# One pool of eight PSUM banks for the whole first phase, and the sample group's products in float32 in quarters of TensorE's columns

## The chip, the core and the metric

The kernel runs on one core of a Trainium2 chip. The metric is the device time of one execution in microseconds (us). The work is spread over TensorE (PE, matmuls and transposes; PEld is its weight load), VectorE (DVE), ScalarE (ACT), GpSimd (POOL) and the queues that issue transfers. TensorE writes its results into PSUM, which has eight banks; a bank holds 128 partitions by 512 float32 values.

## The reference

One step of a two-layer decoder. Layer 0 is sparse attention: an indexer scores all earlier positions, the 256 best are kept, and attention runs over those alone. Layer 1 is a gated linear recurrence (RG-LRU). Two groups go through both layers: a prompt of 2048 tokens, and a sample group of 8 sequences with 4 new tokens each (32 rows), whose 16384 past positions lie in a paged cache.

```python
def attn_project(h, pos, w_in, q_norm, k_norm):
    z = h @ w_in                       # (tokens, 1024) @ (1024, 3664)
    q, k, v, qi, ki, wi, g = jnp.split(z, offs, axis=-1)
    ...
def indexer_select(qi, wi, ki, q_pos, k_sel):
    dots = jnp.einsum('thd,ld->thl', qi, ki)
    score = jnp.einsum('th,thl->tl', wi, jax.nn.relu(dots))
    ...
    _, idx = lax.top_k(score, k_sel)
...
out = (hs * jax.nn.silu(g)) @ w_out    # end of layer 1, (tokens, 1024) @ (1024, 1024)
```

Both groups use the same weights, so each weight matrix is multiplied with 2048 prompt rows and with 32 sample rows.

## The kernel before

The program has three phases. In phase A all tokens are projected by `attn_w_in` (1024 by 3664). The columns are cut into eight groups (`GROUPS`, 384, five times 512, twice 360 columns), the prompt into two halves of eight tiles of 128 tokens. For each group `load_w` fetches the weights (`wraw`), and splits them into a rounded part `whi` and a rest `wlo`; the tokens are split into `hhi` and `hlo` in the same way. A product in full precision is then three fast matmuls (`mm3`: whi with hhi, wlo with hhi, whi with hlo), summed over eight blocks of rows: 24 matmuls into one bank, named `zps`. `make_h` builds hhi and hlo from the prompt's rows: a load (`x`, three buffers), a square sum, two scalings, eight transposes (`htr`).

The sample group has its own chain at the head of phase A. `sample_in` multiplies its rows with the first three groups (`szps`); `sample_scores` then works through 16384 cached indexer keys for each of 8 sequences: 64 gathers of 512 KB (`s_raw`, two buffers), each of them cut into two rounds of four transposes (`s_tp`), a copy by ScalarE (`s_kT`), four products (`s_dots`) and two passes of VectorE (`s_r`, `SC`), 128 rounds in all. `sample_threshold` (names with `st_`) finds the 256th best score by a few steps of a search, and `sample_select` (names with `ss_`, the last matmuls are `ss_ohps`) lists the chosen positions. Only after these three does the program text come to `project`, which holds the prompt's products; into it `weave` lets the sample's attention (`attend`, names with `sa_`), the second layer's conditioning (`ada1`, `aps`) and the first indexer blocks of the prompt (`dots`) in at given shares of its progress.

The order on each engine isn't written by hand. A scheduler places the instructions by their place in the program, and lets a later one go ahead when the earlier ones wait for their inputs; an instruction that writes a new tile needs a free buffer of that tile's pool and tag. The banks of phase A are dealt out like this, by pools and tags:

```python
pps = es.enter_context(tc.tile_pool(name="a_ps", bufs=2, space=PSUM))       # z: 2 banks, tr: 1
pss = early.enter_context(tc.tile_pool(name="a_ps1", bufs=3, space=PSUM))   # st: 3, sd: 2, sample chain
    ps = pps.tile([P, 512], F32, tag="z", name="zps")                       # prompt's projection
    tp = pps.tile([P, 4, P], F32, tag="st", name="s_tp")                    # sample_scores, its pps is a_ps1
```

The pool a_ps1 is followed by a_ps2 for `attend` and by a_ps3 and a_ps4 for the indexer, five banks each.

Phase B is the prompt's attention; its last part (`first_chunk`) also starts layer 0's output product (`ops`, and `sops` for the sample rows). Phase C is the recurrence, in four chunks of 512 tokens. In the first of them each product has a companion for the sample rows: `columns` (`sps`, input weights), `sample_gate` inside `gates` (`sps`, the two gate matrices, fed by `sample_lru`'s `sl_xh` and `sl_xl`), and `row_gemm` in `lru_out` (`sops`). All of these are `mm3` with 32 columns of stationary operand, one after the other with the prompt's matmuls. `load_split` gives their weights, with three (phase B) or four (phase C) buffers of `wraw`.

Of the kernel before, what the change touches and what calls it, by code (L numbers as in the profile page):

```python
# [22 lines left out]
P = 128  # L23
# [47 lines left out]
def _constants():  # L71
# [13 lines left out]
    c["tk_c"] = cf  # L85
    c["iota9"] = np.tile(np.arange(9, dtype=np.float32), (P, 1))
# [7 lines left out]
    for order in (  # L94
        ["ident", "causal", "tk_z", "tk_c", "tk_h", "iota9"],
        ["s_lt", "s_nm", "s_rt", "s_slot", "iota256"],
    ):
# [102 lines left out]
def setup(k, ctx, tc):  # L200
# [21 lines left out]
    k.ogT = [k.cp.tile([P, H, RS], F32R, tag=f"ogT{j}", name=f"ogT{j}") for j in range(2)]  # L222
# [88 lines left out]
def load_w(k, src, row_stride, c0, w, wpool, engs, sub):  # L311
# [3 lines left out]
    for kk in range(0, KT, 2):  # L315
# [7 lines left out]
        out.append((hi, lo))  # L323
    return out

# [64 lines left out]
def sample_h(k, li, x, pool, pps, tag, ptag="tr", mod=None):  # L390
# [22 lines left out]
    hi = k.pp.tile([P, KT, RS], F32R, tag=f"{tag}hi", name=f"{tag}hi")  # L413
    lo = k.pp.tile([P, KT, RS], F32R, tag=f"{tag}lo", name=f"{tag}lo")
    split_ps(k, hi, lo, ps)
    return hi, lo
# [15 lines left out]
def sample_evac(k, gi, ps, pool):  # L432
    nc = k.nc
    a, b = GROUPS[gi]
    if gi == 0:
        z = k.s_ki
        nc.scalar.copy(z[:, 0, :], ps[:, 0:ID])
        nc.scalar.mul(k.s_w, ps[:, WI0 - a : WI0 - a + IH], 1.0 / 32.0)
# [3 lines left out]
    elif gi in (1, 2):  # L442
        z = k.s_qi[:, (gi - 1) * 8 : gi * 8, :]
        nc.scalar.copy(z, ps.rearrange("p (h d) -> p h d", d=ID))
        rope(k, nc.gpsimd, z, 8, ID, k.rope_s, pool, RS)
        return
    elif gi in (3, 4, 5):
# [3 lines left out]
        nc.scalar.copy(z, ps.rearrange("p (h d) -> p h d", d=HD))  # L451
# [20 lines left out]
    nc.scalar.activation(g[:, :n], ps[:, off : off + n], AF.Silu, bias=0.0, scale=1.0)  # L472
# [359 lines left out]
def sample_attend(k, pool, pps):  # L832
# [67 lines left out]
    def output(b, s_ps, vs):  # L900
# [41 lines left out]
        og = pool.tile([P, 2, 4, TD], F32, tag="sa_og", name="sa_og")  # L942
        g = tr["g"][:, :, bt].rearrange("p (v h) t -> p v h t", v=2)
        for kv in range(2):
            V.tensor_tensor(og[:, kv], ot[:, kv, :, 0:4].rearrange("p t h -> p h t"), g[:, kv], ALU.mult)
        og = og.rearrange("p v h t -> p (v h) t")
        nc.scalar.copy(k.ogT[0][:, :, bt], og)
        V.tensor_tensor(k.ogT[1][:, :, bt], og, k.ogT[0][:, :, bt].bitcast(F32), ALU.subtract)
# [38 lines left out]
def phase_a(k):  # L987
    nc, tc = k.nc, k.tc
    with ExitStack() as es:
# [17 lines left out]
        pps = es.enter_context(tc.tile_pool(name="a_ps", bufs=2, space=PSUM))  # L1007
# [13 lines left out]
        with tc.tile_pool(name="a_hs", bufs=1, side="right") as hsp:  # L1021
# [5 lines left out]
            with tc.tile_pool(name="a_ada", bufs=2, side="right") as ap, tc.tile_pool(name="a_pb", bufs=3, space=PSUM) as pss:  # L1027
                cond_t(k, ap, pps)
                for _ in ada(k, 0, ("s", "b"), 512, ap, pps, "z", (10, 3), mod, pss):
                    pass  # L1030
# [13 lines left out]
        early = ExitStack()  # L1044
        pss = early.enter_context(tc.tile_pool(name="a_ps1", bufs=3, space=PSUM))
# [12 lines left out]
        early.close()  # L1058
# [3 lines left out]
        def project():  # L1062

            for hf in range(2):
# [7 lines left out]
                for gi, (a, b) in enumerate(GROUPS):  # L1072
# [4 lines left out]
                    for tiles in TOGETHER:  # L1077
                        ps = [pps.tile([P, 512], F32, tag="z", name="zps")[:, : b - a] for _ in tiles]
                        for kk in range(KT):
                            wk = [t[:, kk % 2, : b - a] for t in w[kk // 2]]  # L1080
# [20 lines left out]
        def index():  # L1101
# [539 lines left out]
def load_split(k, wpool, src, i, bufs=(5, 10)):  # L1641
# [9 lines left out]
    nc.gpsimd.tensor_tensor(lo, raw, hi.bitcast(F32), ALU.subtract)  # L1651
    return hi, lo
# [18 lines left out]
def sample_out(k, li, ps, sl, x, y, pool):  # L1671
# [4 lines left out]
    nc.vector.tensor_tensor(g, ps, g, ALU.mult)  # L1676
# [18 lines left out]
def sample_lru(k, nb, ps_in, gemm_gate, pool):  # L1695
# [9 lines left out]
    xh, xl = t("xh", F32R), t("xl", F32R)  # L1705
# [10 lines left out]
    V.tensor_copy(xh, xc)  # L1716
    V.tensor_tensor(xl, xc, xh.bitcast(F32), ALU.subtract)
    ps_ri = gemm_gate((xh, xl))
# [20 lines left out]
    V.tensor_tensor(gg, gg, i, ALU.mult)  # L1739
    V.tensor_copy(k.s_uT[0][:, fs, :], gg)  # L1740
    V.tensor_tensor(k.s_uT[1][:, fs, :], gg, k.s_uT[0][:, fs, :].bitcast(F32), ALU.subtract)
# [63 lines left out]
def first_chunk(k, pps, tag, spool, mpool):  # L1805
# [9 lines left out]
    with tc.tile_pool(name="c_w0", reuse_waits="tile", bufs=2, side="right") as pool:  # L1815
# [9 lines left out]
        for c in range(0, D, 256):  # L1825
# [3 lines left out]
            pss = pps.tile([P, 512], F32, tag=tag, name="sops")[:RS, :256]  # L1829
            for k0 in range(0, KT, 2):  # L1830
                w = load_split(k, pool, wblock(k.a["attn_w_out"], D, k0, c, 2, 256), k0 // 2, (3, 3))
                for kk in (k0, k0 + 1):
# [5 lines left out]
                    mm3(k, pss, (k.ogT[0][:, kk, :], k.ogT[1][:, kk, :]), wk, kk == 0, kk == KT - 1)  # L1838
# [13 lines left out]
def phase_c(k):  # L1852
    nc, tc = k.nc, k.tc
    V = nc.vector
    with ExitStack() as es:
# [8 lines left out]
        k.s_uT = [one.tile([P, KT, RS], F32R, tag=f"s_u{n}", name=f"s_u{n}") for n in "hl"]  # L1864
# [282 lines left out]
```

## Time and profile before

| | before |
|---|---|
| median of 3 runs (lowest to highest), us | 3037.86 (3033.24 to 3044.44) |
| the profiled execution: its time, its span, us | 3037.36, 3035.6 |
| mean granted TensorE clock | 0.964 |
| busy: PE, PEld, DVE, ACT, POOL | 93%, 78%, 70%, 54%, 41% |
| moved by DMA | 314 MB, 103 GB/s |

The span is what the trace covers; 1.8 us of the execution lie around it. Busy shares are means over stages with different limits, and a matmul's end is modelled: matmuls overlap, so the spacing of their starts is what one costs in a stream, not its duration.

### The profile page before, as it was taken

What the parts mean: (1) busy time and instruction counts of PE and PEld (TensorE: products, weight loads), DVE (VectorE), ACT (ScalarE), POOL (GpSimd) and SP (SyncE); (2) the same over time, 40 slices, a digit from 0 to 9 for tenths busy, and PEclk for the clock granted to TensorE, in tenths of its full rate; (3) what the DMA queues carried; (4) which work ended last, traced back from release to release, by engine and by line L of the source; (5) the groups of instructions that cost most, each with busy time, mean ns of one, the idle gap of its engine ahead of it and who ended that gap; (6) DMA issues with size and microseconds to landing.
All of it is one profiled execution on the core that took longest, in us unless ns stands there. A gap on an engine that the chain in (4) does not pass through costs nothing. (4 is left out here: it accounts for less than half of the span.)

```text
span 3035.6 us, 46937 instructions
## 1 busy us (share of the span) xinstructions
PE 2837.9 (93%) x16289; PEld 2380.2 (78%) x16289; DVE 2115.0 (70%) x4600; ACT 1643.0 (54%) x3083; POOL 1241.8 (41%) x1277
## 2 busy tenths in 40 slices
PE   7999998899999998899999999999997998998998
PEld 2999886687677896788878888888775787787886
DVE  6765568945555876886888787634586487487587
ACT  5533332454443566777877776644464365365364
POOL 2644435515761542422342332124433643653643
PEclk7999999899999998999999999999998999999999
DMA  7554421145663113100110111143322522623523
GB/s 245 185 164 157 148 87 51 59 128 170 205 204 109 64 62 96 58 25 19 39 31 27 31 43 32 53 131 107 111 67 87 198 92 94 204 92 95 177 87 105
DMA packets 202014, 314.13 MB, mean 103 GB/s; under 512 B 25651, under 2 KB 119487, under 8 KB 201758
## 3 DMA queue, kind: packets, MB, share of 16 engines
q1 hardware_dynamic: 151482, 213.72, 22.3%
q0 software_dynamic: 15792, 51.92, 5.6%
q10 hardware_dynamic: 34484, 45.34, 4.6%
q8 instruction: 129, 2.11, 0.3%
q14 instruction: 127, 1.04, 0.1%
HBM read 254.56 MB, written 56.34 MB: 102 GB/s over the span
## 5 line engine op out<-in xcount | busy, mean ns | idle before, releaser
L1651 POOL TENSOR_TENSOR wlo<-wraw,whi 128x512 fp32r<-128x512 f32 x288 | 408.9, 1430 | 477.7 <-ACT whi L1650 430.8
L1230 DVE SCALAR_TENSOR_TENSOR score<-relu,sg_all,score 128x512 f32<-128x512 f32 (+2 forms) x494 | 362.3, 736 | 82.7 <-ACT relu L1222 63.4
L331 PE MATMUL zps<-whi,hhi 128*128 128x512 f32 (+2 forms) x1024 | 389.9, 382 | 15.0 <-ACT z_q L365 9.8
L332 PE MATMUL zps<-wlo,hhi 128*128 128x512 f32 (+2 forms) x1024 | 388.5, 380 | 0.0
L333 PE MATMUL zps<-whi,hlo 128*128 128x512 f32 (+2 forms) x1024 | 387.4, 379 | 0.0
L1222 ACT ACTIVATE relu<-dots 128x512 f32<-128x512 f32 (+2 forms) x608 | 314.5, 551 | 133.7 <-PE dots L1219 76.2
L1455 PE MATMUL o_ps<-v,pt 128*128 128x128 f32 x2176 | 300.9, 278 | 7.4 <-ACT pt L1467 6.7
L1650 ACT CAST whi<-wraw 128x512 fp32r<-128x512 f32 x288 | 175.2, 618 | 242.7 <-PE ops L333 112.1
L1455 PEld LDWEIGHTS o_ps<-v,pt 128*128 128x128 f32 x2176 | 284.6, 193 | 25.5 <-ACT pt L1467 11.6
L1218 PE MATMUL dots<-ki_hi,qiT 128*128 128x512 f32 (+2 forms) x608 | 248.9, 412 | 13.7 <-ACT relu L1222 11.1
L331 PEld LDWEIGHTS zps<-whi,hhi 128*128 128x128 f32 x1024 | 195.7, 191 | 49.3 <-ACT z_q L365 11.9
L1219 PE MATMUL dots<-ki_lo,qiT 128*128 128x512 f32 (+2 forms) x608 | 226.6, 374 | 0.0
L332 PEld LDWEIGHTS zps<-wlo,hhi 128*128 128x128 f32 x1024 | 195.8, 191 | 28.1 <-issue 1.2
L333 PEld LDWEIGHTS zps<-whi,hlo 128*128 128x128 f32 x1024 | 195.5, 191 | 28.1 <-issue 0.8
L1467 ACT COPY pt<-pt_ps 128x512 f32<-128x512 f32 (+3 forms) x320 | 163.7, 527 | 82.4 <-PE pt_ps L1465 77.2
L331 PE MATMUL zps<-hhi,whi 128*128 128x512 f32 x512 | 201.3, 393 | 1.2 <-ACT whi L1650 1.2
L332 PE MATMUL zps<-hlo,whi 128*128 128x512 f32 x512 | 200.9, 392 | 0.0
L333 PE MATMUL zps<-hhi,wlo 128*128 128x512 f32 x512 | 199.2, 390 | 0.0
L189 POOL TENSOR_TENSOR rs<-ms,mhalf 128x1 f32<-128x1 f32 (+4 forms) x85 | 82.3, 970 | 283.3 <-DVE ms L188 274.0
L1442 ACT ACTIVATE sp<-sp,neg 128x128 f32<-128x128 f32 (+15 forms) x128 | 154.3, 1207 | 66.7 <-POOL neg L1441 64.9
L1465 PE MATMUL pt_ps<-const,sp 128*128 128x128 f32 x1088 | 173.0, 274 | 3.6 <-ACT sp L1442 3.1
L555 ACT COPY s_kT<-s_tp 128x512 f32<-128x512 f32 x128 | 75.1, 587 | 165.7 <-PE s_dots L564 134.4
(584 smaller groups left out, 7271.0 us busy)
## 6 DMA issues: line engine op xcount, KB each, us to landing
wraw<-in_lru_w_in SPq DMA_DIRECT2D x128, 256.0 KB
wraw<-in_attn_w_out SPq DMA_DIRECT2D x64, 256.0 KB
wraw<-in_lru_w_out SPq DMA_DIRECT2D x64, 256.0 KB
wraw<-in_attn_w_in SPq DMA_DIRECT2D x28, 512.0 KB
wraw<-in_attn_w_in ACTq DMA_DIRECT2D x20, 512.0 KB
ada_raw<-in_ada_w SPq DMA_DIRECT2D x16, 512.0 KB
qi_d<-z_qi SPq DMA_DIRECT2D x32, 256.0 KB
q_d<-z_q SPq DMA_DIRECT2D x32, 256.0 KB
```

What stands on the lines that cost most here:

```text
L331: mm(ps, ah, bh, start=start, stop=False)
L332: mm(ps, ah, bl, start=False, stop=False)
L333: mm(ps, al, bh, start=False, stop=stop)
L1218: nc.tensor.matmul(ps[:, :w], q, k.ki_hi[:, c : c + w], start=True, stop=False)
L1219: nc.tensor.matmul(ps[:, :w], q, k.ki_lo[:, c : c + w], start=False, stop=True)
L1222: nc.scalar.activation(r[:, :w], ps[:, :w], AF.Relu, bias=0.0, scale=1.0)
L1230: eng.scalar_tensor_tensor(acc, r[:, :w], sg, acc, ALU.mult, ALU.add)
L1455: nc.tensor.matmul(u.o[:, j, :], pt[:, i, :], k.v_sb[k0 + i][:, u.kv * HD : (u.kv + 1) * HD], start=(k0 + i == 0), stop=(k0 + i == u.qt),)
L1465: nc.tensor.transpose(pt_ps[:, i, :], sp[:, (k0 + i) * P : (k0 + i + 1) * P], k.ident)
L1467: nc.scalar.copy(pt[:, :n, :], pt_ps[:, :n, :])
L1650: nc.scalar.copy(hi, raw)
L1651: nc.gpsimd.tensor_tensor(lo, raw, hi.bitcast(F32), ALU.subtract)
```

## The change

All PSUM tiles of phase A come from one pool of eight buffers. A small class `Banks` passes every request on under the one tag `bank`; the three extra pools are gone. The sample group's rows stay in float32 (`hsT`, `ogT`, `s_uT` lose their split halves), and so do the weights that they meet (`wraw` itself, which is kept until its product has been taken). `mm_rows` makes four matmuls of a quarter of the columns each, which write to partitions 0, 32, 64 and 96 of one bank; in `columns` and `sample_gate` the four quarters are two blocks of rows times two halves of the columns, or two matrices times two halves. What evacuates such a bank does it in four pieces, or by one matmul that sums and transposes (`s_sel`).

```diff
-        out.append((hi, lo))
+        out.append((hi, lo, raw))
+def mm_rows(k, ps, rows, w, start, stop):
+    n = w.shape[1] // 4
+    for q in range(4):
+        k.nc.tensor.matmul(ps[q * RS : (q + 1) * RS, :n], rows, w[:, q * n : (q + 1) * n], start=start, stop=stop)
...
 def sample_in(k, gi, w, pool, pps):
     a, b = GROUPS[gi]
-    hi, lo = k.hsT
-    pst = pps.tile([P, 512], F32, tag="z", name="szps")
-    ps = pst[:RS, :]
+    ps = pps.tile([P, 512], F32, tag="z", name="szps")
     for kk in range(KT):
-        wh, wl = w[kk // 2]
-        mm3(k, ps[:, : b - a], (hi[:, kk, :], lo[:, kk, :]), (wh[:, kk % 2, : b - a], wl[:, kk % 2, : b - a]), kk == 0, kk == KT - 1)
+        mm_rows(k, ps, k.hsT[:, kk, :], w[kk // 2][2][:, kk % 2, : b - a], kk == 0, kk == KT - 1)
...
-        pps = es.enter_context(tc.tile_pool(name="a_ps", bufs=2, space=PSUM))
+        pps = Banks(es.enter_context(tc.tile_pool(name="a_ps", reuse_waits="tile", bufs=8, space=PSUM)), 8)
...
-        early = ExitStack()
-        pss = early.enter_context(tc.tile_pool(name="a_ps1", bufs=3, space=PSUM))
+        pss = pps
...
         def attend():
-            with (
-                tc.tile_pool(name="a_sa", reuse_waits="tile", bufs=2, side="right") as ssp,
-                tc.tile_pool(name="a_ps2", reuse_waits="tile", bufs=2, space=PSUM) as pss,
-            ):
-                yield from sample_attend(k, ssp, pss)
+            with tc.tile_pool(name="a_sa", reuse_waits="tile", bufs=2, side="right") as ssp:
+                yield from sample_attend(k, ssp, pps)
...
-            with (
-                tc.tile_pool(name="a_ps3", reuse_waits="tile", bufs=4, space=PSUM) as pd,
-                tc.tile_pool(name="a_ps4", reuse_waits="tile", bufs=1, space=PSUM) as pq,
-            ):
-                for i in range(0, NT, 4):
-                    prep_index(k, i, pq, "q")
-                    yield 1024
-                yield from indexer(k, tiles, GP_HEADS[0], k.first, k.ip, k.ip, k.ip, "scoreA", pd, "dots", "q", pq)
+            for i in range(0, NT, 4):
+                prep_index(k, i, pps, "q")
+                yield 1024
+            yield from indexer(k, tiles, GP_HEADS[0], k.first, k.ip, k.ip, k.ip, "scoreA", pps, "dots", "q")
...
-                    mm3(k, pss, (k.ogT[0][:, kk, :], k.ogT[1][:, kk, :]), wk, kk == 0, kk == KT - 1)
+                    mm_rows(k, pss, k.ogT[:, kk, :], raw[:, kk - k0, :], kk == 0, kk == KT - 1)
...
-                    mm3(k, pss[:RS, :], (sample[0][:, kk, :], sample[1][:, kk, :]), w[kk], kk == 0, kk == KT - 1)
+                    mm_rows(k, pss, sample[:, kk, :], k.raw[:, 0, :], kk == 0, kk == KT - 1)
...
-                    if u.sample:
-                        mm3(
-                            k, u.sps[:RS, part * 256 : part * 256 + 256], (k.hsT[0][:, kk, :], k.hsT[1][:, kk, :]),
-                            [t[:, kk - k0, :] for t in w], part + kk == 0, part * kk == KT - 1,
-                        )
+                if u.sample:
+                    for j in range(2):
+                        for n in range(2):
+                            p0 = (j * 2 + n) * RS
+                            nc.tensor.matmul(
+                                u.sps[p0 : p0 + RS, part * P : (part + 1) * P], k.hsT[:, k0 + n, :],
+                                raw[:, n, j * P : (j + 1) * P], start=(k0 == 0), stop=(k0 == KT - 2),
+                            )
...
+class Banks:
+    def __init__(self, pool, n):
+        self.pool, self.n = pool, n
+    def tile(self, shape, dt, tag=None, name=None, bufs=None):
+        return self.pool.tile(shape, dt, tag="bank", name=name, bufs=self.n)
```

On TensorE, in the middle of the scoring (`sample_scores`), the order before has the prompt's `zps` between the sample's rounds:

```order
L331 MATMUL zps<-whi,hhi 128x512
L553 MATMUL s_tp<-const,s_raw 128x128
L564 MATMUL s_dots<-bd,s_kT 128x128 x4
L553 MATMUL s_tp<-const,s_raw 128x128 x2
L564 MATMUL s_dots<-bd,s_kT 128x128 x4
L553 MATMUL s_tp<-const,s_raw 128x128 x5
L332 MATMUL zps<-wlo,hhi 128x512
L333 MATMUL zps<-whi,hlo 128x512
```

In the changed kernel the same place, the start of the scoring on TensorE, reads (the line numbers have moved by some 13):

```order
L334 MATMUL szps<-wraw,hs_474 32x128 x8
L514 MATMUL s_qps<-const,s_qi 128x32 x12
L545 MATMUL s_nps<-bd,s_kn 4x64 x8
L566 MATMUL s_tp<-const,s_raw 128x128 x8
L577 MATMUL s_dots<-bd,s_kT 128x128 x4
L566 MATMUL s_tp<-const,s_raw 128x128 x4
L577 MATMUL s_dots<-bd,s_kT 128x128 x4
```

The last two rows go on in turn to the end of the 128 rounds, and no `zps` and no `htr` stands between them.

At the end of the selection on TensorE, the order before again alternates; `ss_oh` and `ss_ohps` are the sample's, `zps` the prompt's:

```order
L818 LDWEIGHTS ss_oh
L818 MATMUL ss_ohps<-ss_R,ss_oh 128x130
L331 MATMUL zps<-whi,hhi 128x360
L332 MATMUL zps<-wlo,hhi 128x360
L333 MATMUL zps<-whi,hlo 128x360
L331 MATMUL zps<-whi,hhi 128x360
L332 MATMUL zps<-wlo,hhi 128x360
L818 LDWEIGHTS ss_oh
L818 MATMUL ss_ohps<-ss_R,ss_oh 128x130
```

In the changed kernel the last `ss_ohps` is followed by the transposes of the first eight prompt tiles, and then by the first `zps` of the program:

```order
L831 LDWEIGHTS ss_oh
L831 MATMUL ss_ohps<-ss_R,ss_oh 128x130
L308 MATMUL htr<-const,x 128x128 x64
L341 MATMUL zps<-whi,hhi 128x384
L342 MATMUL zps<-wlo,hhi 128x384
L343 MATMUL zps<-whi,hlo 128x384
```

The prompt's projection has moved behind the sample's whole chain. The 64 transposes of the second half of the prompt (`htr`) likewise stand in one block behind the last `zps` of the first half, where before they alternated with that half's last `zps`.

In phase C, chunk 0, TensorE's order before has three matmuls for the sample (`sps`) behind each six of the prompt:

```order
L333 MATMUL zps<-hhi,wlo 128x512
L331 MATMUL sps<-whi,hs1hi 32x256
L332 MATMUL sps<-wlo,hs1hi 32x256
L333 MATMUL sps<-whi,hs1lo 32x256
L331 MATMUL zps<-hhi,whi 128x512
```

In the changed kernel four quarter matmuls (`hs` is the sample's rows in float32) stand behind each twelve of the prompt:

```order
L343 MATMUL zps<-hhi,wlo 128x512
L1941 MATMUL sps<-wraw,hs_27539 32x128 x4
L341 MATMUL zps<-hhi,whi 128x512
```

Six matmuls with 256 columns have become four with 128.

## Rows read from the trace of the kernel before

**Rows 1.** The page: busy time of the engines, TensorE's granted clock in 40 slices
```profile
PE 2837.9 (93%) x16289; PEld 2380.2 (78%) x16289; DVE 2115.0 (70%) x4600; ACT 1643.0 (54%) x3083; POOL 1241.8 (41%) x1277
PEclk7999999899999998999999999999998999999999
```

**Rows 2.** Busy time of each engine by stretch, with granted clock and DMA
```profile
core 0: us, PE busy (x) PEld busy (x) DVE busy (x) ACT busy (x) POOL busy (x), PEclk, DMA share, GB/s
...
98.00:425.00 327.00, 326.52 (x2260) 297.60 (x2257) 204.45 (x334) 113.85 (x207) 134.67 (x174) 1.00 0.47 147
425.00:500.00 75.00, 71.52 (x308) 53.34 (x308) 56.16 (x230) 23.38 (x35) 42.95 (x51) 0.98 0.26 80
500.00:634.00 134.00, 111.21 (x566) 89.73 (x565) 121.56 (x256) 65.52 (x217) 61.98 (x55) 0.90 0.19 59
...
2110.00:2330.00 220.00, 185.33 (x949) 146.50 (x948) 158.25 (x272) 122.94 (x216) 85.85 (x62) 0.91 0.27 87
```

**Rows 3.** The same view for the tile zps alone, 75 to 634 us
```profile
75.00:634.00 559.00, 333.56 (x1398) 253.55 (x1399) 1.33 (x8) 33.86 (x74) 0.97 0.39 120
```

**Rows 4.** Groups of instructions, 98 to 425 us: count, busy us, mean ns, idle before
```profile
L572 DVE TENSOR_REDUCE SC<-s_r 128x32 f32<-128x512 f32 x128 | 87.9, 688 | 4.0
L570 DVE SCALAR_TENSOR_TENSOR s_r<-s_dots,s_wb 128x512 f32<-128x512 f32 x128 | 87.8, 687 | 101.4 <-PE s_dots L564 100.8
```

**Rows 5.** TensorE's instructions in order of time, one round of the scoring
```profile
300.67 0.40 PE L333 MATMUL zps<-whi,hlo 128*128 128x512 f32 x1
300.91 0.27 PE L553 MATMUL s_tp<-const,s_raw 128*128 128x128 f32 x1
301.02 1.06 PE L564 MATMUL s_dots<-bd,s_kT 128*128 128x128 f32 x8
301.91 0.38 PE L553 MATMUL s_tp<-const,s_raw 128*128 128x128 f32 x2
```

**Rows 6.** DMA issues: engine, count, median us from issue to landing
```profile
x<-in_x_prompt POOLq DMA_DIRECT2D x3, 512.0 KB, 5.0
s_raw<-in_cache_idx_k,s_idx POOLq DMA_INDIRECT x64, 4.6
```

**Rows 7.** Groups of VectorE, 425 to 500, then 500 to 634; ScalarE, 574 to 634
```profile
L375 DVE SCALAR_TENSOR_TENSOR z_q<-z_q,rs,qn 128x128 f32<-128x128 f32 x24 | 7.5, 370 | 0.2 <-POOL rs L189 0.2
L371 DVE TENSOR_REDUCE ssq<-sq 128x4 f32<-128x512 f32 (+1 forms) x9 | 5.3, 588 | 7.5 <-ACT sq L369 7.5
...
L375 DVE SCALAR_TENSOR_TENSOR z_q<-z_q,rs,qn 128x128 f32<-128x128 f32 x40 | 13.0, 383 | 1.9 <-POOL rs L189 1.9
L371 DVE TENSOR_REDUCE ssq<-sq 128x4 f32<-128x512 f32 x10 | 6.6, 665 | 1.5 <-ACT sq L369 1.5
...
L822 ACT ACTIVATE ss_junk<-ss_ohps,const_s 128x128 bf16<-128x128 f32 x64 | 23.6, 369 | 7.3 <-PE ss_ohps L818 6.4
L822 ACT ACTIVATION_READ_ACCUMULATOR ss_junk<-ss_ohps,const_s 128x1 f32 x64 | 12.7, 198 | 0.0
```

**Rows 8.** Instructions of the tile x: ns min/median/max, first and last start
```profile
L299 DVE SCALAR_TENSOR_TENSOR x<-x,rs,s_bc x16: 1274/1284/3405, 63.7 to 700.8; 128x1024 f32<-128x1024 f32 x16
...
L300 POOL TENSOR_TENSOR x<-x,b_bc x8: 2347/2394/2997, 68.7 to 124.8; 128x1024 f32<-128x1024 f32 x8
```

**Rows 9.** TensorE in order of time: quarter products of the sample's attention
```profile
767.97 1.08 PE L933 MATMUL sa_o<-sa_v,sa_pT 128*32 128x128 f32 x32
768.88 0.60 PE L895 MATMUL sa_s<-sa_kT,sa_qz 128*32 128x256 f32 x4
769.41 0.76 PE L886 MATMUL sa_ktp<-const,sa_k 128*128 128x128 f32 x5
```

**Rows 10.** TensorE in order of time: a sample product in phase C and what follows it
```profile
2193.53 0.28 PE L333 MATMUL sps<-whi,hs1lo 128*32 128x256 f32 x1
2193.65 0.40 PE L331 MATMUL zps<-hhi,whi 128*128 128x512 f32 x1
```

**Rows 11.** Who waited for whom, TensorE: us in total, times, longest
```profile
PE sps L331 <- DVE sl_xh L1716: 23.1, 3, 19.6
```

More of the change, by code (lines that the diff above doesn't have):

```diff
@@ L221, in setup @@
     k.sg_d = k.dr.tile([RS, D], F32, tag="sg_d", name="sg_d")
-    k.ogT = [k.cp.tile([P, H, RS], F32R, tag=f"ogT{j}", name=f"ogT{j}") for j in range(2)]
+    k.ogT = k.cp.tile([P, H, RS], F32, tag="ogT", name="ogT")
     k.sg_all = cp.tile([P, NT, IH], F32, tag="sg_all", name="sg_all")
@@ L434, in sample_evac @@
     a, b = GROUPS[gi]
+    n4 = (b - a) // 4
+    quarters = [ps[q * RS : (q + 1) * RS, :n4] for q in range(4)]
     if gi == 0:
         z = k.s_ki
-        nc.scalar.copy(z[:, 0, :], ps[:, 0:ID])
-        nc.scalar.mul(k.s_w, ps[:, WI0 - a : WI0 - a + IH], 1.0 / 32.0)
+        nc.scalar.copy(z[:, 0, :], quarters[0][:, 0:ID])
+        nc.scalar.mul(k.s_w, quarters[0][:, WI0 - a : WI0 - a + IH], 1.0 / 32.0)
         rope(k, nc.gpsimd, z, 1, ID, k.rope_s, pool, RS)
@@ L443, in sample_evac @@
         z = k.s_qi[:, (gi - 1) * 8 : gi * 8, :]
-        nc.scalar.copy(z, ps.rearrange("p (h d) -> p h d", d=ID))
+        for q in range(4):
+            nc.scalar.copy(z[:, q * 2 : q * 2 + 2, :], quarters[q].rearrange("p (h d) -> p h d", d=ID))
         rope(k, nc.gpsimd, z, 8, ID, k.rope_s, pool, RS)
@@ L450, in sample_evac @@
         z = zt[:RS]
-        nc.scalar.copy(z, ps.rearrange("p (h d) -> p h d", d=HD))
+        for q in range(4):
+            nc.scalar.copy(z[:, q, :], quarters[q])
         sqt = pool.tile([P, nh, HD], F32, tag="sq", name="ssq", bufs=1)
@@ L471, in sample_evac @@
     g = gt[:RS]
-    nc.scalar.activation(g[:, :n], ps[:, off : off + n], AF.Silu, bias=0.0, scale=1.0)
+    for q in range(4):
+        at = max(off, q * n4)
+        to = (q + 1) * n4
+        nc.scalar.activation(g[:, at - off : to - off], quarters[q][:, at - q * n4 :], AF.Silu, bias=0.0, scale=1.0)
     c0 = a + off - G0
@@ L1675, in sample_out @@
     nc.sync.dma_start(g, k.s_ada[li, "gate"][:, sl])
-    nc.vector.tensor_tensor(g, ps, g, ALU.mult)
+    n = (sl.stop - sl.start) // 4
+    for q in range(4):
+        gq = g[:, q * n : (q + 1) * n]
+        nc.vector.tensor_tensor(gq, ps[q * RS : (q + 1) * RS, :n], gq, ALU.mult)
     nc.vector.tensor_tensor(y, g, x, ALU.add)
@@ L1863, in phase_c @@
         V.tensor_copy(k.s_xb[:, :, :, 0:3], k.s_old)
-        k.s_uT = [one.tile([P, KT, RS], F32R, tag=f"s_u{n}", name=f"s_u{n}") for n in "hl"]
+        k.s_uT = one.tile([P, KT, RS], F32, tag="s_u", name="s_u")
         pool = es.enter_context(tc.tile_pool(name="c_w", reuse_waits="tile", bufs=2))
@@ L1877, in row_gemm @@
             ps = [px.tile([P, 512], F32, tag="z", name="ops") for _ in range(4)]
-            pss = pz.tile([P, 512], F32, tag="z", name="sops") if sample else None
+            pss = pz.tile([P, 512], F32, tag="z", name="sops") if sample is not None else None
             w = []
@@ L1985, in gate, with sample_gate, sample_x @@
                     mm3(k, ps, [t[:, kk, j * P : (j + 1) * P] for t in wg[q]], x[kk], kk == 0, kk == 1)
[L1987 to L2002 removed]
+            def sample_gate(x):
+                for kk in range(2):
+                    for q in range(2):
+                        for j in range(2):
+                            p0 = (q * 2 + j) * RS
+                            nc.tensor.matmul(
+                                u.sps[p0 : p0 + RS, :P], x[:, kk, :], raws[q][:, kk, j * P : (j + 1) * P],
+                                start=(kk == 0), stop=(kk == 1),
+                            )
+                z = pool.tile([P, 512], F32, tag="xh", name="sl_z")[:, :P]
+                nc.scalar.copy(z, u.sps[:, :P])
+                t = u.spt[:, 1]
+                nc.tensor.transpose(t.rearrange("p q j t -> p (q j t)"), z, k.ident)
+                return t
+            def sample_x():
+                z = pool.tile([P, 512], F32, tag="xh", name="sl_z")[:, : 2 * P]
+                nc.scalar.copy(z, u.sps[:, : 2 * P])
+                t = u.spt[:, 0]
+                for part in range(2):
+                    nc.tensor.matmul(t[:, part].rearrange("p j t -> p (j t)"), z[:, part * P : (part + 1) * P], k.s_sel, start=True, stop=True)
                 return t
```

67 lines of the change are left out of this document (23 added, 44 removed).

## The prediction

> **What bounds the kernel now.** I read the head of the page first [rows 1]: TensorE is busy 93% of the span at a clock near full. Only the first slice stands clearly lower (7 tenths of the clock), so there is little waiting to remove. Then the table by stage [rows 2], cut where the sample's chain changes its step: 98 to 425 us is the scoring (the first of its 128 rounds to the last), 425 to 500 the threshold, 500 to 634 the selection. TensorE is busy 326.5 of 327, 71.5 of 75 and 111.2 of 134 us there. The reader is to see that this isn't the sample's own work: the tile `zps`, the prompt's projection, fills 333.6 us of it with 1398 matmuls [rows 3]. Without that filler the three stages are a chain of gathers, VectorE and small ScalarE steps. VectorE works 687 and 688 ns in each round, 176 us in 128 rounds, and sat idle 101 us before `s_r`, waiting for `s_dots`, since TensorE was at the filler [rows 4]. So the first 634 us hold two long things side by side: the sample's chain, bound by latency, and the projection, bound by TensorE.
>
> **The change, part 1: the banks.** What decides is the order on TensorE, shown in the section on the change. One tag means that banks are dealt out in program order. The sample's chain stands ahead of `project` in the program, so no `zps` and no `htr` is placed before the last `ss_ohps`. An engine runs its rows in order. What lay side by side is now one behind the other, and I add it up along TensorE's order.
>
> *The chain alone.* Its first product comes at 98 us now [rows 2]. A few `htr` and `zps` ahead of it fall away; I take 95.
> Scoring: a round's own TensorE time is 0.89 us (eight passes of `s_dots`, 301.02 to 301.91) and four transposes of 0.11 us, 1.33 us [rows 5]; VectorE's is 1.375 us [rows 4], so 176 us is the lower end. What isn't seen today is the pace of the gathers, because TensorE is slower than they are. A gather lands 4.6 us after its issue [rows 6], and there are two buffers. One is held while its eight transposes and the products between them run (0.44 + 0.89 + 0.44 = 1.8 us, from [rows 5]) and the last transpose ends (0.27); with some 0.15 for the handover a buffer turns round in 6.8 us. Two buffers, 64 gathers: 32 turns of 6.8 are 218 us. That is also longer than the rounds need (four of 1.375 us per turn, 5.5), so I take it. Scoring ends at 313.
> Threshold and flag: 75 us now, in which VectorE also did the projection's norms, 7.5 and 5.3 us and some small ones [rows 7]. Its own chain is serial with TensorE and ScalarE, so little beyond that falls away: 57.
> Selection: 134 us now, VectorE busy 121.6 [rows 2], of which 13.0 and 6.6 are norms [rows 7] and about 11 are small ones and second-half rows. The last part is ScalarE's, 23.6 and 12.7 us in `ss_ohps` [rows 7], not shortened. I take 97.
> The chain ends at 95 + 218 + 57 + 97 = 467 us, against 634 now.
>
> *Then the start of the projection.* The 64 `htr` follow. `x` has three buffers, so three of the eight tiles can be ready; the other five come in two waves, and each needs a load (5.0 [rows 6]), a square sum, a scaling (1.28) and an addition on GpSimd (2.39 [rows 8]), eight transposes (0.9 by [rows 5]) and handovers, some 12 us a wave: 25 us, in which TensorE's own work is 7. Before, this was hidden behind the scoring.
> *Then the filler.* The 1398 matmuls cost 0.234 us each at 512 columns (300.67 to 300.91 [rows 5]) and less in proportion at 384 and 360. By the program's widths (192 of 384, 960 of 512, the rest of 360) that is 299 us; the upper end is the 333.6 of [rows 3], which has their tails. The sample's products of groups 3 to 7, now 40 sets of quarters, add 8. So where TensorE stands today at 634 it now stands at 467 + 25 + 307 = 799: **+165**.
> *Middle of the projection.* The second block of 64 `htr` repeats the start with VectorE in GpSimd's place; a little conditioning lies beside it: **+20** (0 if the rows are ready early).
> *The rest of phase A.* `zps`, `sa_` and `dots` now alternate in coarser pieces, but eight banks let TensorE run ahead. The kept `wraw` delays one load per group: the fourth of three buffers waits for the first products. The load takes about 5 us, as `x` with the same 512 KB [rows 6]; the order puts some 26 `zps` (6 us) in that place, which hide it. Without that cover it is 5 us in five groups. I take **+10** for both, 0 to 35.
>
> **Part 2: the quarters.** The trace has such products in the sample's attention: 32 passes with 128 columns from 767.97 to 768.88 [rows 9], 0.23 us for four float32 products of two passes, which run beside each other. The three matmuls that a set replaces cost 0.70 us at 512 columns and 0.35 at 256 (spacing 0.12 [rows 10]). In `first_chunk`, 32 sets of 64 columns: 0.35 against 0.11 to 0.23, -6. In `columns`, 32 sets against six matmuls of 256 (0.70): -15; `sample_gate`, 8 sets: -4; `lru_out`, 16 sets: -7.5. The 19 us of `columns` and `sample_gate` lie in a stretch where TensorE is busy 185 of 220 us, VectorE 158 [rows 2], and TensorE waited 23.1 us for `sl_xh` in the sample's recurrence [rows 11]; what TensorE saves there it partly waits longer, and I take half. Sum: -6 - 10 - 7 = **-23**, between -10 and -33. Evacuations in four pieces and the splits left out lie on ScalarE and VectorE beside TensorE's work in these stages and count as nothing; if ScalarE were late they would cost a few hundred ns per group.
>
> **The sum.** The profiled execution took 3037.4 us, a span of 3035.6 and 1.8 around it; the median of the runs is 0.5 higher, so nothing is to be corrected. 3037 + 165 + 20 + 10 - 23 = **3209**, and I say 3210.
>
> **Rivals.**
> *Half clock in the scoring.* Alone, TensorE works 5.3 of every 6.8 us there. Where it is busy 83 to 84% of a stretch, the granted clock was 0.90 and 0.91, with long waits in it; where it was fed without gaps, 1.00 [rows 2]. The gaps would be short here, which speaks against. If all of the scoring ran at 1.2 GHz instead of 2.4, a round would be 2.66 us of TensorE and 128 of them 340 us, 122 more than 218: 3330.
> *A drain at each change between quarters and the whole array.* The price of one would be a matmul's duration less its spacing, 0.27 - 0.11 = 0.16 us [rows 5]; the 88 sets after the first phase with two changes each would lose 28 us and eat part 2 whole: about 3240. Against it: from quarter products to whole transposes (768.88 to 769.41 [rows 9]) four passes of 256 columns in two pairs of about 0.21 leave 0.1 at most, and a 32-column product is followed by a whole one at 0.12 [rows 10]. The Trainium skill, page "TensorEngine Tiling (Array Packing)", section "Tiling Modes" (Key Properties), says that changing the tiling mode drains TensorE; by that this rival would hold, and the rows show at most a small part of it.
> *Faster.* The chain alone would have to be so short that the lost cover costs less than part 2 brings. By the sum it decides at 467 - 172 = 295 us: chain over by then. From 95 that leaves 200 us for scoring, threshold and selection, while VectorE alone needs 176 for the scoring [rows 4] and about 40 and 85 for the other two [rows 2, 7]. At 280 us the time would be 3022. Nothing in the profile speaks for it.
> *The change doesn't do what it says* (banks shared, projection still between the rounds): it would gain the 23 us and the six or so of the sample's products, about 2990. The order, which is the program, excludes it.
>
> **How the numbers follow.** Forecast 0.81, half clock over much of the scoring 0.13, drain 0.03, faster (either way) 0.02, no change 0.01. The range: at the lower end the scoring runs at VectorE's pace (-42) and the two blocks of `htr` are half hidden (-22), with the rest at its middle, 3145, and 15 below for a chain that starts earlier; at the upper end half the clock rival (+60) and the late loads (+25), 3295. So 3130 to 3300. A difference of 0.5% (15 us) is about what a measurement of this kernel can tell from no change. Slower 0.97, same 0.01, faster 0.02.
>
> **What would show it.** In the changed kernel's trace the last `ss_ohps` should stand near 467 us and the first `zps` near 490, none before; TensorE's busy share should be about 80% in the scoring and a few per cent in threshold and selection, with a low clock there. A pair of gathers should take 6.8 us; `s_tp` should wait for `s_raw`. From the first `zps` on, the trace should be that of before, later by about 195 at the end of phase A and by some 172 at the end. Four quarters should take 0.23 us. The prediction is wrong if `zps` starts before 400 us (gathers faster, or stages shorter than their rows) or after 560 (clock), or if attention and indexer in the rest of phase A lose tens of us in the coarser order.

## The result, and the profile after

The changed kernel takes 3239.91 us (median of 4 runs, 3233.24 to 3243.18), the kernel before beside it 3037.57: the ratio is 1.0663, with a 95% interval of 1.0645 to 1.0681. It is slower, as forecast, and by 6.6% in place of 5.7%: 30 us above the predicted 3210. The profiled execution took 3233.24 us, so the two traces are 196 us of span apart; that is what the tables below divide up.

The page's head of the changed kernel, to be set against [rows 1]: the engines' busy time, and TensorE's granted clock in 40 slices.

```profile
PE 2825.8 (87%) x16917; PEld 2370.7 (73%) x16917; DVE 2106.7 (65%) x4592; ACT 1652.3 (51%) x3105; POOL 1205.5 (37%) x1277
...
PEclk7799659999898999999999999999998999999999
```

TensorE has as much to do as before (2826 against 2838 us) in a span that is 196 us longer (3231.5 against 3035.6). What was lost is its waiting: 406 us idle against 198. So the question of the whole comparison is where TensorE now stands still. The table by stage answers it (columns as in [rows 2]); the cuts are the first `s_dots`, the ends of scoring, threshold and selection, the first `zps`, the last `szps`, the last `htr`, the first `dots`, and the start of phase B.

```profile
0.00:118.00 118.00, 57.37 (x333) 26.74 (x333) 56.21 (x71) 50.87 (x94) 34.22 (x35) 0.67 0.54 179
118.00:332.00 214.00, 179.45 (x1532) 172.63 (x1532) 161.45 (x254) 74.33 (x127) 58.10 (x62) 0.99 0.52 154
332.00:379.00 47.00, 4.62 (x25) 2.81 (x23) 36.66 (x180) 2.30 (x4) 0.56 (x1) 0.58 0.00 1
379.00:459.00 80.00, 14.93 (x72) 6.76 (x72) 76.96 (x173) 35.46 (x135) 0.00 (x0) 0.50 0.00 0
459.00:493.00 34.00, 15.09 (x62) 12.16 (x63) 22.25 (x35) 20.45 (x65) 15.68 (x10) 0.55 0.48 149
493.00:803.00 310.00, 310.00 (x1708) 261.58 (x1708) 79.26 (x187) 82.82 (x152) 149.00 (x211) 0.99 0.27 88
803.00:858.00 55.00, 39.43 (x234) 37.31 (x233) 28.13 (x40) 23.96 (x46) 9.21 (x16) 0.82 0.44 140
858.00:1155.00 297.00, 254.50 (x1606) 203.28 (x1604) 127.76 (x349) 110.32 (x220) 136.92 (x141) 0.91 0.53 159
1155.00:1398.00 243.00, 239.27 (x1157) 205.21 (x1157) 184.99 (x412) 130.89 (x226) 83.00 (x82) 0.99 0.20 64
```

Span less PE busy is the idle time. Added up it is 283 us at the start of phase B, 60.6 of it ahead of the chain, 161 in the chain and the `htr` block behind it (34.6, 42.4, 65.1, 18.9), none in the projection, 15.6 in the second `htr` block, 42.5 in the attention and the indexer's preparation. The same cuts in the trace of before:

```profile
0.00:98.00 98.00, 74.95 (x291) 37.93 (x292) 62.38 (x77) 55.25 (x97) 39.60 (x41) 0.81 0.74 242
98.00:423.00 325.00, 324.52 (x2252) 295.93 (x2248) 202.57 (x329) 113.85 (x207) 134.11 (x172) 1.00 0.48 148
...
634.00:712.00 78.00, 68.09 (x389) 62.27 (x388) 34.53 (x76) 27.92 (x62) 6.84 (x15) 0.93 0.39 125
712.00:993.00 281.00, 275.85 (x1674) 210.03 (x1673) 149.08 (x404) 116.54 (x224) 150.36 (x143) 0.98 0.58 178
```

There the start has 23 us of it, the scoring 0.5, the second `htr` block 9.9 and the stretch behind it 5.2; threshold and selection have 26 together, and the whole up to phase B 68. The difference, 215 us, with 7 more of work, is the 222 us by which phase B starts later (first `kps` 1397.8 against 1175.8). Up to its `first_chunk` (first `ops` 2215.1 against 2012.3), phase B gives 19 back (8 of them in its first 102 us, where TensorE idles 11 us and idled 19 before), the rest of the program 7. That leaves 196. Why phase B is shorter isn't shown; `e2_banks` below, without quarters, gives back 18 there as well, so it isn't the quarters' doing.

The waits of TensorE at the start say what it stood at (columns as in [rows 11]):

```profile
PE szps L334 <- DMA wraw<-in_attn_w_in: 19.6, 9, 6.8
PE bcps L284 <- DVE mrow L277: 14.2, 2, 8.4
...
PE bcps L284 <- DVE mrow L273: 6.1, 2, 4.0
```

The `bcps` are the broadcasts of the conditioning. Before, they had a pool of their own (L282) and cost 2.4 us of waiting; now 20 us pass in front of them. That the `aps` products behind them could run meanwhile is a guess here; `e11_bc_apart` tests it.

### The profile page after: what moved, and what is told of

It is laid out like the page before. It is cut to its first block, busy times and chain, and to the rows that moved or that the text cites. A ratio compares the mean times of both kernels' runs of the same rounds, so it can differ in the third digit from the quotient of the medians.

```text
span 3231.5 us, 48473 instructions
## 1 busy us (share of the span) xinstructions
PE 2825.8 (87%) x16917; PEld 2370.7 (73%) x16917; DVE 2106.7 (65%) x4592; ACT 1652.3 (51%) x3105; POOL 1205.5 (37%) x1277
## 3 DMA queue, kind: packets, MB, share of 16 engines
q14 instruction: 125, 1.02, 0.1%
```

## The experiments

The kernel before took 3038 us beside e1 to e4, and on another chip 3079 beside e5 to e8 and 3083 beside e9 to e11. So a time is compared with the kernel before, or the changed kernel, of its own set alone; ratios carry over better than times (the changed kernel's is 1.0663 in the first set and 1.0631 in the last).

### One half of the change each

`e1_quarters` keeps the four pools of before and takes only the second part of the change:

```diff
-        pps = Banks(es.enter_context(tc.tile_pool(name="a_ps", reuse_waits="tile", bufs=8, space=PSUM)), 8)
+        pps = es.enter_context(tc.tile_pool(name="a_ps", bufs=2, space=PSUM))
...
-        pss = pps
+        early = ExitStack()
+        pss = early.enter_context(tc.tile_pool(name="a_ps1", bufs=3, space=PSUM))
```

> Only the second part of the change: the four pools of PSUM banks as before, the sample's products as float32 quarters. Theory (the whole loss lies in dealing the banks in program order): the chain stays between the projection's matmuls, the last ss_ohps stands at 615 to 650 us, and the time is 3010 to 3040 us: minus 9 to 25 us from the shorter products, plus up to 20 us at the start, where the weights that are kept until their product has been taken hold back the next loads. Rival A (quarters cost: a drain at each change of tile shape, or kept weights that stall every group): 3060 us or more, with gaps of 0.15 us and more around each set, or waits for wraw in groups 3 to 7.

Measured: 3037.2 us beside 3037.76, ratio 0.9999 (0.9988 to 1.001). In the whole the second part is worth nothing, where 23 us had been put down for it. The time lies in the expected range, but the gaps of rival A around each set are there, too (last experiment): from the first `ops` on, this trace is 7 us shorter than that of before, and its chain starts 6 us later (first `s_dots` at 104.3 against 98.6 us).

`e2_banks` is the kernel before with the one pool and the one tag, and with `mm3` for the sample as before (the same lines, the other way round).

> Only the first part of the change: one pool of eight banks under one tag, the sample's products as three fast matmuls of split operands as before. Theory: the full loss stays, 3220 to 3265 us (ratio to before 1.06 to 1.075); no zps before the last ss_ohps; the scoring takes 205 to 225 us. If the kept weights delay the chain's start in the changed kernel, the first s_dots stands here near 98 to 105 us instead of 118. Rival A (a good part of the loss is due to the quarters): 3040 to 3150 us.

Measured: 3236.73 us, ratio 1.066 (1.0642 to 1.0678). The whole loss is here. Its first `s_dots` stands at 114.8 us; without kept weights the chain starts only 3 us earlier than in the changed kernel, so the second half of this expectation (98 to 105) was wrong: the late start belongs to the banks, too.

### Is it the one pool or the one tag?

`e3_two_tags` has the pool of eight banks and splits the tag:

```diff
-        return self.pool.tile(shape, dt, tag="bank", name=name, bufs=self.n)
+        own = tag in ("z", "tr")
+        return self.pool.tile(shape, dt, tag="project" if own else "bank", name=name, bufs=3 if own else 5)
```

> The changed kernel with its one pool of eight banks, dealt under two tags: three banks for the projection (zps, szps, htr, aps), five for all else. Theory (one tag binds the projection behind the chain): overlap is back, the chain and half of the projection share the time up to some 640 to 680 us, and the whole takes 3010 to 3080 us. Rival B (it is the pool itself, its single space or its way of waiting for a buffer, that costs): 3200 us or more.

Measured: 3055.97 us, ratio 1.006 (1.0046 to 1.0074). Its table for scoring, threshold and selection has TensorE at 362 of 367, 69.6 of 70 and 101.5 of 133 us:

```profile
103.00:470.00 367.00, 361.99 (x2500) 328.52 (x2499) 200.44 (x339) 120.78 (x220) 151.20 (x194) 0.99 0.46 141
470.00:540.00 70.00, 69.61 (x362) 55.05 (x359) 64.43 (x237) 19.74 (x33) 36.69 (x49) 1.00 0.17 59
540.00:673.00 133.00, 101.51 (x651) 89.39 (x650) 108.72 (x229) 63.67 (x200) 48.50 (x36) 0.86 0.25 75
673.00:725.00 52.00, 26.57 (x129) 23.81 (x128) 28.47 (x49) 22.50 (x59) 15.26 (x22) 0.60 0.40 123
```

Two lines bring back nine tenths of the loss. The pool is innocent; what binds is that two independent strands of work draw from one tag. Of the 18 us that stay lost, the larger part is seen in the last row: TensorE idles 25 us in the second `htr` block (9.9 before); in the three rows above it, it idles 37 (27 before). That `htr` and `zps` still share a tag would explain the last row, but wasn't tried.

### Does the order of the program alone decide?

`e4_woven` leaves the one tag alone and changes the program's text: `sample_scores`, `sample_threshold` and `sample_select` become a generator that yields (after each round, each search step and the like), and `weave` deals it into the projection:

```diff
+        early = chain()
+        next(early)
...
             [
+                (early, 500, 0.0, 0.43),
                 (attend(), NB * (TD + 1), *A_ATTEND),
```

> The changed kernel with its one pool and its one tag, but the program text in another order: the sample's scoring, threshold and selection are a generator which the existing weave deals into the projection's progress (share 0 to 0.43 of it), as it does for attention and indexer. Theory (one tag deals banks in the order of the program, and nothing but that order matters): 3020 to 3110 us, with zps between the rounds and the last ss_ohps at 560 to 680 us. Rival B (one tag or one pool costs by itself, whatever the order): 3180 us or more.

Measured: 3197.69 us, ratio 1.0531 (1.0511 to 1.0551): inside the rival's range, and the last `ss_ohps` stands at 745.8 us, later than the theory's 560 to 680. In the scoring the order was as meant, 816 `zps` lay inside it; yet only 42 us came back. So the theory in its plain form failed, and the trace had to say why. Waits of TensorE, 547 to 746 us (threshold and selection):

```profile
PE ss_selps L790 <- DVE ss_csel L787: 15.9, 1, 15.9
PE ss_eqps L770 <- DVE ss_ceq L768: 14.8, 1, 14.8
PE st_tp L631 <- DVE st_C L627: 12.9, 1, 12.9
PE st_bps L680 <- DVE st_e L673: 11.2, 1, 11.2
```

TensorE's queue stands at a product of the chain, with no `zps` placed in between. The projection handed over only after 24 or 48 matmuls. `e8_woven_fine` makes it hand over after every block of rows:

```diff
                                 mm3(k, p, [t[:, kk, :] for t in hs[n]], wk, kk == 0, kk == KT - 1)
+                            yield (b - a) * len(tiles) / KT
...
-                        for _ in tiles:
-                            yield b - a
```

> The woven kernel (one pool, one tag, the sample's chain dealt into the projection), with the projection handing over after each block of rows, six or three matmuls, in place of after each 24 or 48. Theory (what the woven order still lacks is its coarse grain, TensorE's queue standing at a product of the chain with no zps dealt in between): 3060 to 3130 us. Rival (with one tag a bank is dealt only after all earlier tiles had theirs, so nothing can fill a wait of the chain, however fine the order): 3165 to 3205 us, with TensorE idle in threshold and selection for some 60 to 75 us as in the coarse one.

Measured: 3146.84 us beside 3078.57, ratio 1.0219 (1.0185 to 1.0254). In us that lies between the two ranges, but they were set by the times of the first chip. As a share of the time of before, 5.3% of loss became 2.2%, so the grain of the order was more than half of what was missing, as the theory had it. The rival's sign, idle time in threshold and selection, is there as well. The table for scoring (from the first `zps` on), threshold and selection:

```profile
152.00:512.00 360.00, 359.64 (x2493) 325.64 (x2492) 198.87 (x341) 118.16 (x214) 145.87 (x196) 0.99 0.45 137
512.00:567.00 55.00, 33.78 (x145) 25.91 (x143) 48.82 (x204) 12.66 (x19) 22.98 (x25) 0.84 0.07 24
567.00:697.00 130.00, 90.61 (x567) 73.84 (x567) 112.97 (x246) 59.90 (x196) 55.11 (x51) 0.85 0.17 55
```

In the scoring TensorE is hardly idle now. In threshold and selection it still is, 61 us (26 before), of which 29.2 in one wait of `ss_selps` for `ss_csel`: whoever writes the order by hand has to guess how long VectorE will take there. With tags of their own the strands don't need that guess. Another part of the rest lies ahead of the table: the chain starts as late as in the changed kernel (first `s_dots` at 120.0 us), and the first `zps` comes at 152.4. So the order explains more than half of the loss; that a finer order would bring back all of it isn't shown.

### What sets the pace of the scoring alone?

`e5_sraw3` is the changed kernel with a third buffer for the gathers:

```diff
-                raw = pool.tile([P, 1024], F32, tag="s_raw", name="s_raw")
+                raw = pool.tile([P, 1024], F32, tag="s_raw", name="s_raw", bufs=3)
```

> The changed kernel with three buffers of s_raw in place of two, nothing else. Theory (alone, the scoring goes at the pace of two gathers in 6.7 us, since a buffer is held until its transposes are done): with three buffers the gathers would need 64 x 6.7 / 3 = 143 us, less than VectorE's 176, so VectorE and TensorE set the pace: scoring 176 to 192 us against 214, and the whole 22 to 38 us shorter than the changed kernel, 3202 to 3218 us. Rival (the pace is that of the issue on GpSimd or of the serial steps of a round): scoring still 205 us or more, time 3230 to 3245 us.

Measured: 3232.76 us, ratio 1.0502 (1.0468 to 1.0536), scoring 170 us. The time lies in the rival's range, which was set for the first chip, but the scoring is 35 us below the rival's and 6 below the theory's. Since its set ran on a slower chip, it was repeated beside the changed kernel:

> The changed kernel once more, as the reference on one chip for the two kernels beside it: the chip that ran the third set took 1.3% longer for the kernel before, so times of different sets can't be set against each other. Ratio to before 1.05 to 1.068; scoring 214 us.

> Three buffers of s_raw beside the changed kernel on the same chip. The scoring took 170 us with them where the changed kernel took 214 on another chip. If that lies on the path that sets the end, as the sum of the prediction has it, the whole is 35 to 45 us shorter than the changed kernel beside it; if something behind the chain (loads, the gathers of the sample's attention) was waited for anyway, 0 to 25.

Measured in that set: the changed kernel 3278.23 us, ratio 1.0631 (1.0606 to 1.0656); with three buffers 3228.21, ratio 1.0471 (1.0448 to 1.0494). In the changed kernel GpSimd, which issues the gathers, waits for the transposes to free a buffer (waits, 122 to 338 us):

```profile
POOL s_raw L560 <- PE s_tp L566: 146.9, 60, 5.4
```

and the scoring takes 216 us with TensorE busy 180.8. With the third buffer it takes 170, all of them busy:

```profile
122.00:292.00 170.00, 170.00 (x1529) 169.97 (x1529) 158.54 (x253) 74.43 (x127) 57.34 (x61) 1.00 0.65 191
```

The 46 us of the scoring come back whole in the time (50 us, 5 more than the upper end expected; the runs of either kernel spread over 5 to 7 us): once the chain runs alone, its pace is the kernel's. VectorE is busy 158.5 us there with all but a few of 256 passes, some 1.25 us a round and not 1.375, since passes that follow each other overlap in the record.

### Why the chain starts late

`e11_bc_apart` gives the `bcps` two banks under a tag of their own and six to all else (the same line of `Banks` as in `e3_two_tags`).

> The changed kernel with two tags: two banks for the conditioning's broadcasts (bcps), six for all else. Theory (at the start TensorE's queue stands at a bcps whose row isn't ready, while aps products could run): the first s_dots at 100 to 110 us against 118, and the whole 8 to 18 us shorter than the changed kernel on the same chip, if six banks are as good as eight behind it. Rival (the late start is due to the weights that are kept and loaded later): first s_dots at 115 us or later, same time.

Measured: 3266.87 us against 3278.23 of the same set. The first `s_dots` moved from 121.6 to 100.8 us, and of the 21 us the whole kept 11. The lead is still 19 us at the first `dots` (1180.3 against 1199.4); it shrinks behind it, and why wasn't tried.

### What a change between quarters and the whole array costs

The timeline of the changed kernel in `lru_out`, one set among the prompt's matmuls:

```profile
2564.63 0.40 PE L342 MATMUL ops<-wlo,uhi 128*128 128x512 f32 x1
2564.86 0.40 PE L343 MATMUL ops<-whi,ulo 128*128 128x512 f32 x1
2565.19 0.42 PE L334 MATMUL sops<-wraw,s_u 128*32 128x128 f32 x8
2565.55 0.50 PE L341 MATMUL ops<-whi,uhi 128*128 128x512 f32 x1
2565.88 0.40 PE L342 MATMUL ops<-wlo,uhi 128*128 128x512 f32 x1
```

Among themselves the prompt's matmuls follow each other after 0.23 us. Here the set starts 0.33 after the matmul ahead of it, and the matmul behind it holds up the next one 0.33 instead of 0.23. From 2564.86 to 2565.88 are 1.02 us; less two spacings of 0.234, the set costs **0.55 us**, not 0.23. `e6_grouped` puts two sets together where the order lets it, in `first_chunk` (shown), `columns` and `lru_out`, and takes the pools and the first phase's products back to before. So against `e1_quarters` it changes two things:

```diff
-                    mm_rows(k, pss, k.ogT[:, kk, :], raw[:, kk - k0, :], kk == 0, kk == KT - 1)
+                    if kk > k0:
+                        for n in (0, 1):
+                            mm_rows(k, pss, k.ogT[:, k0 + n, :], raw[:, n, :], k0 + n == 0, k0 + n == KT - 1)
```

> The kernel before with its four pools and its split products in the first phase, and with float32 quarters only where the weights meet them in first_chunk, columns, sample_gate and lru_out; there two sets are issued one behind the other where the order allows it, so that TensorE changes between quarters and the whole array half as often. Theory (each change to and fro costs 0.33 us, a set itself 0.22): 10 us less in columns, 5 in lru_out, 2 in first_chunk, of which part is waited longer elsewhere; time 3019 to 3030 us, ratio 0.994 to 0.9975. Rival (a set costs its 0.55 us whatever stands beside it): no better than quarters in single sets, 3033 to 3040 us.

Measured: 3063.61 us beside 3078.57, ratio 0.995 (0.9932 to 0.9968). It beats both kernels, the only one that does. From the first `ops` on its trace is 13 us shorter than that of before, where single sets bring 7 (these stages take the changed kernel 1016.4 us on either chip). So grouping is worth some 6 us, not the 17 that the expectation starts from: in `columns` the order leaves many sets single. The first phase, too, is that of before again. A pair of sets in its trace:

```profile
2399.14 0.40 PE L343 MATMUL ops<-whi,ulo 128*128 128x512 f32 x1
2399.47 0.64 PE L334 MATMUL sops<-wraw,s_u 128*32 128x128 f32 x16
2400.04 0.50 PE L341 MATMUL ops<-whi,uhi 128*128 128x512 f32 x1
2400.38 0.40 PE L342 MATMUL ops<-wlo,uhi 128*128 128x512 f32 x1
```

A pair of sets of 128 columns costs 0.77 us (median of six in `lru_out`: 1.240 from the matmul ahead to the second one behind, less 0.467), against 0.55 for a single one. A set is worth 0.22, then, and the change to and fro 0.33, whether one set or two stand between. `e7_one_quarter` asks what the change hangs on:

```diff
-                    mm_rows(k, pss, sample[:, kk, :], k.raw[:, 0, :], kk == 0, kk == KT - 1)
+                    nc.tensor.matmul(pss[:RS, :], sample[:, kk, :], k.raw[:, 0, :], start=kk == 0, stop=kk == KT - 1)
```

> The kernel with only the second part of the change; in lru_out of the recurrence's first chunk the four quarter products of a set become one float32 product with 512 columns in the first quarter alone. It tells what the change to and fro hangs on. If on products that lie in several quarters: a set is entered 0.23 us after the matmul before it and left at a matmul's usual spacing, the matmul behind it is not late, and the set costs its passes alone, 0.47 to 0.95 us. If on float32 products with 32 columns of stationary operand as such: entered after 0.32 us, left with the matmul behind it 0.1 us late, as in the quarters.

```profile
2418.89 0.40 PE L343 MATMUL ops<-whi,ulo 128*128 128x512 f32 x1
2419.22 1.05 PE L1893 MATMUL sops<-wraw,s_u 128*32 128x512 f32 x2
2420.19 0.50 PE L341 MATMUL ops<-whi,uhi 128*128 128x512 f32 x1
2420.53 0.40 PE L342 MATMUL ops<-wlo,uhi 128*128 128x512 f32 x1
```

Entered after 0.33 us and left with a late successor, though only one quarter is used: the second answer. Several quarters aren't needed for it; a float32 product with 32 columns of stationary operand is enough. The sample's fast matmuls of before, also with 32 columns, didn't pay it ([rows 10]: 0.12 from one to the next), nor do whole float32 transposes ([rows 5]: 0.24 and then 0.11). The time of this kernel (3098.13) is a single one and isn't used.

## Why the prediction was right, and where it wasn't

**The order decides: right.** None of the projection ran before the chain had ended (last `ss_ohps` at 458.5 us, forecast 467; first `zps` at 493.3, forecast about 490), and `e2_banks` has the whole loss. Of the stages, scoring took 214 us (218), threshold and flag 47 (57), selection 80 (97). The reason given for the scoring's pace, two buffers that turn round in 6.8 us (6.7 measured), is shown by `e10_sraw3_again`; the lower end, though, was TensorE's 1.33 us a round (170 us), not VectorE's 176.

**The start of the chain: 95 predicted, 118 measured.** I let a few `htr` and `zps` fall away and overlooked that the setup's broadcasts lose their own banks as well. `e11_bc_apart` shows it: with banks of their own for the broadcasts, the chain starts at 100.8 us.

**+165 for the chain, the first `htr` block and the filler: +171 measured**, at the 1398th `zps`, up to which the sum counts (633.9 to 805.2 us). The chain's end was 8 us early, the block 35 us instead of 25, and the filler 312 instead of 307. In the block TensorE waited 18.4 us for the additions of GpSimd (`x`), as described. Its transposes ran at a granted clock of 0.55 after the long idle stretch, which the 25 us didn't count; how much of the 10 us that was, wasn't tried.

**Second block and the rest of phase A: 20 + 10 predicted, 51 measured** (222 at the start of phase B, less 171). The second `htr` block cost 6 us of idle time, not 20. The stretch behind it cost 37; the other 8 are work that took longer. Its waits, 858 to 1155 us:

```profile
PE sa_ktp L899 <- DMA sa_k<-in_cache_k,s_rows: 19.7, 8, 4.5
PE qips L1188 <- POOL qis L1184: 11.7, 4, 4.5
```

These are the step's own words, "coarser pieces", with a size: the attention's gathers and the indexer's rows are waited for, where TensorE waited 5.1 us for `sa_k` before. That the `zps` in banks of their own filled those waits then is the likely reason, but isn't shown. `e2_banks` idles 31.6 us in that stretch (869 to 1153), so most of it is the banks' doing; which of the tiles that share them, wasn't tried. The range for this term (0 to 35) ended 2 us short of it. Tens of us lost there were named as a sign that the prediction is wrong: in this step it was.

**The quarters: -23 predicted, -7 measured from `first_chunk` on and 0 in the whole of `e1_quarters`; this step failed.** I priced a set at 0.23 us and gave the drain 3 in 100. That rival had its price nearly right (0.32 for the change to and fro; measured 0.33, though not as 0.16 each way: 0.09 at the entry, the rest at leaving). In `lru_out` a set costs 0.55 against 0.70, in `columns` 0.54 against 0.70, and in `first_chunk`, where a set of 64 columns costs 0.45 against 0.34, it loses. Summed over the sets, without those of `sample_gate`, that is 16 x 0.15 + 32 x 0.16 - 32 x 0.11, some 4 us gained. The traces are 7 us shorter from the first `ops` on in the changed kernel as in `e1_quarters`, of which 3 may be chance, since `e2_banks`, without quarters, is 3 shorter there; and in `e1_quarters` phase B starts 4 us later than before. The Trainium skill, page "TensorEngine Tiling (Array Packing)", section "Tiling Modes" (Key Properties), says that changing the mode drains TensorE; the 0.33 us for a pair of changes agree with that, though no row says that it is the mode that changes, and a fast product with 32 columns doesn't pay it. What misled me was the choice of rows. I read quarter products that are followed by transposes [rows 9] and a fast 32-column matmul [rows 10]. The same trace has the change itself, 11 us further on:

```profile
779.10 0.39 PE L333 MATMUL zps<-whi,hlo 128*128 128x512 f32 x1
779.42 0.62 PE L895 MATMUL sa_s<-sa_kT,sa_qz 128*32 128x256 f32 x2
779.97 0.50 PE L331 MATMUL zps<-whi,hhi 128*128 128x512 f32 x1
780.30 0.39 PE L332 MATMUL zps<-wlo,hhi 128*128 128x512 f32 x1
```

0.32 us from the matmul ahead to the float32 product, and 0.33 from the matmul behind it to the next one, where 0.23 is usual: the price stood there, in the very neighbourhood (fast whole matmuls) that the change creates.

**Half clock in the scoring: wrong, as expected.** The granted clock was 0.99 there at 84% busy. It fell to 0.58 and 0.50 in threshold and selection, where TensorE had 20 us to do in 127. **Faster, and no effect:** excluded by the order, and so it came.

One of the rivals' sums was wrong in itself: 3037 less 23 and 6 are 3008, not 2990. Nothing else uses it.

In sum, 165 + 20 + 10 - 23 = 172 was forecast. Measured, the same terms are 171 + 51 - 7 (the stages from `first_chunk` on), and 19 that phase B gave back before, which the sum didn't have: 196. At the end of phase A it is 222, where about 195 was forecast. The mechanism of the large term was right. That the total came as near as it did is in part luck: 6, 21 and 16 us too little in three terms, and 19 the other way that nobody had counted. It is luck, too, that the drain rival's 3240 is the measured time, for it was made of the same terms.

## What to carry to other kernels

In this program a tag works like a queue: its buffers are dealt in program order, and one strand that waits holds up those that come after it. Give each independent strand a tag of its own, even inside one pool; look at the order of the waiting engine before and after, and count what was beside a latency-bound chain and no longer is. And read the price of an operation from a row in which it has the neighbours that it will have.

## What the runs showed of the hardware that was not expected

A set of float32 matmuls with 32 columns of stationary operand costs 0.33 us more than its passes when fast whole-array matmuls stand on both sides (0.55 us for a set, 0.77 for two together); the same product in split fast matmuls costs nothing extra (0.12 us a matmul, [rows 10]), and a pair of sets shares the price. The same program, the kernel before, took 3038 us on one chip and 3079 to 3083 on another, 1.3 to 1.5% more; in the changed kernel the difference lies in the sample's attention (first `sa_tp` to first `dots`: 289 us in the first profile, 327 in the later one), and not in the scoring (214 and 216). Why, isn't shown; the kernel before has no trace on the second chip.
